# Five activation tiles of a two-layer backbone kernel begin 32 bytes further in SBUF

## The chip, the cores and the metric

The kernel runs on one core of a Trainium2 chip. The metric is the device time of one execution in microseconds (us); the time before is the median of three runs. The profile is of one further execution on the chip.

## What is computed

The reference is a diffusion backbone of two layers on 256 latent and 256 context tokens of width 1024, in float32. Each layer is a half-weighted SwiGLU feed-forward step (width 2816), a token mixer (neighbourhood attention, a bidirectional linear recurrence and a Fourier mix behind one input projection and in front of one output projection) and a second feed-forward step. Each step is modulated by columns made from a conditioning vector, and each is followed by a layer norm over the residual. Cut to what matters here:

```python
def swiglu(h, wg, wu, wd):
    return (jax.nn.silu(h @ wg) * (h @ wu)) @ wd

def ffn_sublayer(xs, m, j, wg, wu, wd, g, b):
    y = MACARON * swiglu(modulate(xs, m, j), wg, wu, wd)
    return residual_post_norm(xs, m[3 * j + 2] * y, g, b)

for l in range(DEPTH):
    x_lat = ffn_sublayer(x_lat, m_lat, 0, ...)
    x_ctx = ffn_sublayer(x_ctx, m_ctx, 0, ...)
    y_lat, y_ctx = hybrid_mixer(modulate(x_lat, m_lat, 1), modulate(x_ctx, m_ctx, 1), ...)
    x_lat = residual_post_norm(x_lat, m_lat[5] * y_lat, ...)
    x_lat = ffn_sublayer(x_lat, m_lat, 2, ...)
    ...
```

## The kernel before, in words

Activations are kept transposed: features on the 128 partitions, the 512 tokens (256 of the context, then 256 latent ones) along the free dimension, eight chunks of features one behind the other. A product with a weight matrix is made in three parts so that float32 accuracy is kept with a rounded type: an operand is split into a high part (`hH`, `aH`, `whi`) and a remainder (`hL`, `aL`, `wlo`), and high by high, high by remainder and remainder by high are summed in PSUM. All this is issued by `mmh` at line 420: a matmul there has a block of weights of 128 by 128 as its stationary operand and 256 columns of an activation tile as its moving operand; for every matmul the weights are loaded anew. With both streams, two such matmuls (context, latent) follow each other with the same weights. In the rows, `gu` are the products of the feed-forward steps' two input matrices, `dn` those of their output matrix, `pj`, `head` and `wo` those of projections.

Weights come by DMA in tiles of 128 by 1024 (`raw`), five of them in turn, ScalarE rounds them (`whi`, line 282) and VectorE or GpSimd subtracts (`wlo`, line 620). Their order is a fixed sequence (`seq`), and the order of the mixer's pieces is written out by hand (`ORDER`); neither has to do with addresses.

Where a tile lies in SBUF follows from the order in which the pools and their tiles are made. The pool `const` is the first. Its first tile begins at byte 16,512 of each partition, which leaves 128 when divided by 512. Five tiles of 16,384 bytes follow one another there: `xT` (the residual), `hH` and `hL` (the input of a product), `aH` and `aL` (the input of the next). Then come `cs` (5,632 bytes: the identity matrix and Fourier tables), `vT` (1,536), `onesD` (512), and `one_c` (one column of ones, 4 bytes, which takes 32). All sizes but the last are multiples of 512, so each of these nine begins at remainder 128. Every slice that a matmul of line 420 takes of `hH`, `hL`, `aH` or `aL` begins a multiple of 1,024 bytes into its tile, so it too begins at remainder 128. Behind `one_c` lie small tiles and then the other pools; `raw`, `whi`, `wlo`, the pool `acc` (with the queries of the attention, `q`) and the pool `scr` (with its keys, `k`) all begin at remainder 448, and a weight block of 512 bytes too.

`one_c` is read as a bias of one column, twice in each piece `sq` of the mixer (line 930).

Of the kernel before, what the change touches and what calls it, by code (L numbers as in the profile page):

```python
# [11 lines left out]
F32 = mybir.dt.float32  # L12
# [53 lines left out]
def kernel(ctx: ExitStack, tc: tile.TileContext, x, cx, vecs, cst, bias, w_ada,  # L66
# [3 lines left out]
    const = ctx.enter_context(tc.tile_pool(name="const", bufs=1))  # L70
# [10 lines left out]

    V, S, G, PE = nc.vector, nc.scalar, nc.gpsimd, nc.tensor

    xT = const.tile([128, KD, 512], F32, name="xT")
    hH = const.tile([128, KD, 512], F32R, name="hH")
    hL = const.tile([128, KD, 512], F32R, name="hL")
# [7 lines left out]
    SN = cs[:, 896:1408].rearrange("p (a b) -> p a b", a=2)  # L94
    vT = const.tile([128, V_ROWS], F32, name="vT")
    onesD = const.tile([128, 128], F32, name="onesD")
    one_c = const.tile([128, 1], F32, name="one_c")
    pick = const.tile([128, 2, 2], F32R, name="pick")
    scol = const.tile([128, KD, 2], F32, name="scol")
    bmean = const.tile([128, 6], F32, name="bmean")  # L100
# [1409 lines left out]
```

## Time and profile before

| | |
|---|---|
| median of 3 runs | 1820.0 us (1819.4 to 1820.87) |
| the profiled execution's own time | 1820.95 us |
| its span, first to last instruction | 1819.2 us |
| TensorE matmul busy (PE) | 1729.1 us, 95% |
| TensorE weight load busy (PEld) | 1658.0 us, 91% |
| VectorE busy (DVE) | 1282.1 us, 70% |
| ScalarE busy (ACT) | 742.0 us, 41% |
| GpSimd busy (POOL) | 460.2 us, 25% |
| mean granted TensorE clock | 0.982 of full |
| moved by DMA | 253.32 MB, mean 139 GB/s |

Busy time of an engine is the time in which at least one of its instructions runs; matmuls overlap each other, so their mean durations do not add up to it. How often TensorE can begin a matmul is read from the starts of successive ones, or from a piece of the chain that holds nothing else: its length divided by its count. This distance is called the pitch below.

### The profile page before, as it was taken

The page shows a single profiled execution, that of the slowest core. Times are in us where ns is not written, and L with a number is a line of the kernel's source. Part 1 is how long each engine was busy: PE and PEld are TensorE (multiplying, and loading weights), DVE is VectorE, ACT ScalarE, POOL GpSimd, SP SyncE. Part 2 cuts the span into 40 slices and gives each one's busy share as a digit, 9 for nine tenths or more (in the row PEclk, how much of TensorE's full clock was granted, in tenths as well). Part 3 has the DMA queues.
Part 4 walks back from the last instruction along what each step waited for, and adds up shares of the span by engine and source line. Part 5 has one row for each costly group of instructions (what it writes and reads, how often), then busy time and mean ns, then how long its engine had stood idle before and what let it go on. Part 6 is the DMA issues. An engine that isn't in the chain of part 4 may idle for free.

```text
span 1819.2 us, 33814 instructions
## 1 busy us (share of the span) xinstructions
PE 1729.1 (95%) x14145; PEld 1658.0 (91%) x14145; DVE 1282.1 (70%) x1857; ACT 742.0 (41%) x1191; POOL 460.2 (25%) x326
## 2 busy tenths in 40 slices
PE   6899999999899999999999999999999989989997
PEld 4789999998798899999999989999999878879997
DVE  6899799956685678866565568865653768676565
ACT  4322232233757545422222364223223466655443
POOL 3435133243542044110101140100000466150000
PEclk8999999999999999999999999999999999999999
DMA  8367555643213225644454326665563232357662
GB/s 292 98 187 204 151 171 169 185 126 93 71 47 93 70 71 147 185 140 143 127 172 120 90 59 185 178 183 159 179 184 95 82 105 70 105 158 214 183 198 83
DMA packets 375080, 253.32 MB, mean 139 GB/s; under 512 B 8144, under 2 KB 336336, under 8 KB 374928
## 3 DMA queue, kind: packets, MB, share of 16 engines
q1 hardware_dynamic: 373856, 248.81, 46.4%
q8 instruction: 111, 1.82, 0.4%
q0 software_dynamic: 1072, 2.36, 0.4%
q14 instruction: 41, 0.34, 0.1%
HBM read 250.09 MB, written 1.05 MB: 138 GB/s over the span
## 4 chain that ended last, share of the span: by engine, by line
PE 74%; DVE 17%; ACT 5%; issue 2%; DMA 1%; POOL 0%; SPq 0%; DVEq 0%; ACTq 0%
PE gu L420 39%; PE dn L420 21%; PE head L420 5%; DVE acc L319 3%; PE pj L420 3%; PE wo L420 2%; DVE wlo L620 1%; DVE ri L939 1%; DVE h L1324 1%; PE o L1133 1%; DVE aL L620 1%; DVE xl L906 1%; ACT whi L282 1%; DVE xT L754 1%; PE adap L359 1%
## 5 line engine op out<-in xcount | busy, mean ns | idle before, releaser
L420 PE MATMUL gu<-hH,whi 128*128 128x256 f32 x2336 | 493.8, 281 | 8.3 <-ACT hH L1326 6.8
L420 PE MATMUL gu<-hH,wlo 128*128 128x256 f32 x2336 | 492.2, 280 | 6.8 <-DVE wlo L620 6.4
L420 PE MATMUL gu<-hL,whi 128*128 128x256 f32 x2336 | 492.2, 280 | 1.7 <-POOL hL L620 0.9
L282 ACT CAST whi<-raw 128x1024 fp32r<-128x1024 f32 (+1 forms) x319 | 318.8, 1025 | 177.6 <-PE dn L420 70.8
L420 PEld LDWEIGHTS gu<-hH,whi 128*128 128x128 f32 x2336 | 372.0, 190 | 13.0 <-ACT hH L1326 7.3
L420 PEld LDWEIGHTS gu<-hH,wlo 128*128 128x128 f32 x2336 | 371.9, 190 | 7.8 <-DVE wlo L620 7.2
L620 DVE TENSOR_TENSOR wlo<-raw,whi 128x1024 fp32r<-128x1024 f32 (+2 forms) x250 | 313.2, 1256 | 88.0 <-ACT whi L282 79.9
L420 PEld LDWEIGHTS gu<-hL,whi 128*128 128x128 f32 x2336 | 370.7, 190 | 2.5 <-DVE hL L620 1.4
L620 POOL TENSOR_TENSOR wlo<-raw,whi 128x1024 fp32r<-128x1024 f32 (+2 forms) x110 | 217.0, 1979 | 440.2 <-ACT whi L282 414.8
L319 DVE SCALAR_TENSOR_TENSOR acc<-raw,scol,acc 128x512 f32<-128x512 f32 x337 | 291.4, 912 | 1.0
L420 PE MATMUL dn<-aH,whi 128*128 128x256 f32 x1280 | 285.0, 282 | 6.0 <-DVE xT L754 2.9
L420 PE MATMUL dn<-aL,whi 128*128 128x256 f32 x1280 | 280.7, 279 | 0.3 <-DVE aL L620 0.3
L420 PE MATMUL dn<-aH,wlo 128*128 128x256 f32 x1280 | 280.8, 279 | 0.0
L420 PEld LDWEIGHTS dn<-aH,whi 128*128 128x128 f32 x1280 | 208.4, 189 | 11.1 <-DVE xT L754 4.5
L420 PEld LDWEIGHTS dn<-aH,wlo 128*128 128x128 f32 x1280 | 208.0, 189 | 0.2
L420 PEld LDWEIGHTS dn<-aL,whi 128*128 128x128 f32 x1280 | 207.4, 188 | 0.7 <-DVE aL L620 0.7
L767 ACT CAST aH<-pr 128x512 fp32r<-128x512 f32 (+1 forms) x88 | 50.0, 568 | 369.0 <-DVE pr L766 369.0
L766 DVE TENSOR_TENSOR pr<-sg,gu 128x512 f32<-128x512 f32 (+1 forms) x84 | 51.6, 614 | 166.0 <-PE gu L420 111.1
L754 DVE SCALAR_TENSOR_TENSOR xT<-dn,gate,xT 128x256 f32<-128x256 f32 x174 | 78.0, 478 | 83.5 <-PE dn L420 83.0
L381 POOL TENSOR_TENSOR fold<-fold 128x512 f32<-128x512 f32 x24 | 49.3, 2054 | 267.1 <-DVE fold L313 267.1
L420 PE MATMUL pj<-hH,whi 128*128 128x256 f32 x384 | 84.7, 289 | 5.3 <-ACT pt L1102 2.8
L364 ACT COPY rows<-adap 2x512 f32<-2x512 f32 x31 | 17.5, 575 | 162.2 <-PE adap L359 162.2
(267 smaller groups left out, 2377.4 us busy)
## 6 DMA issues: line engine op xcount, KB each, us to landing
raw<-in_w_ada_dram SPq DMA_DIRECT2D x136, 512.0 KB, 4.6
raw<-in_ff_gate_dram SPq DMA_DIRECT2D x88, 512.0 KB, 4.1
raw<-in_ff_up_dram SPq DMA_DIRECT2D x88, 512.0 KB, 4.7
raw<-in_ff_down_dram SPq DMA_DIRECT2D x64, 448.0 KB, 4.0
raw<-in_w_in_dram SPq DMA_DIRECT2D x36, 512.0 KB, 3.9
raw<-in_ff_down_dram SPq DMA_DIRECT2D x32, 512.0 KB, 4.4
raw<-in_w_out_dram SPq DMA_DIRECT2D x16, 512.0 KB, 3.6
in<-in_w_ada_dram SPq DMA_DIRECT2D x8, 512.0 KB, 6.7
```

Of the source, the lines that this page charges most:

```text
L282: S.copy(h_[:, :n], t[:, :n])
L319: V.scalar_tensor_tensor(out=a[:, st], in0=t[:, kk * 512:(kk + 1) * 512], scalar=sc_, in1=a[:, st], op0=ALU.mult, op1=ALU.add)
L359: PE.matmul(pp[0:2, :], lhsT=pick[:, n - 1], rhs=parts[:, i], start=(i == 0), stop=(i == 1))
L381: G.tensor_tensor(out=a[:, 0], in0=a[:, 0], in1=a[:, 1], op=ALU.add)
L420: PE.matmul(o[:, c], lhsT=w, rhs=X[:, k, c], start=first and i == 0, stop=last and i == len(halves) - 1)
L620: (eng or V).tensor_tensor(out=dst_l, in0=src, in1=dst_h.bitcast(F32), op=ALU.subtract)
L754: V.scalar_tensor_tensor(out=xT[:, j, a:b], in0=ps[:, a:b], scalar=gate[:, st, j:j + 1], in1=xT[:, j, a:b], op0=ALU.mult, op1=ALU.add)
L766: V.tensor_tensor(out=pr[:, c], in0=sg[:, c], in1=up[:, c], op=ALU.mult)
L767: S.copy(aH[:, m, c], pr[:, c])
L906: V.scalar_tensor_tensor(out=t3[:, :, off:], in0=s3[:, :, :256 - off], scalar=w[tp], in1=t3[:, :, off:], op0=ALU.mult, op1=ALU.add)
L939: V.reciprocal(gates[c, d][0], gates[c, d][0])
L1133: PE.matmul(o[c][r, a:b], lhsT=vk[c][:, x_ * 128 + 64 * p_:x_ * 128 + 64 * p_ + 64], rhs=pt[c, p_, h][:, kc * 256:(kc + 1) * 256], start=( ...
```

## The change

`one_c` is made first in the pool instead of ninth. It takes 32 bytes at 16,512, so `xT`, `hH`, `hL`, `aH`, `aL`, `cs`, `vT` and `onesD` begin 32 bytes further, the activation tiles at byte 16,544 and its successors, all at remainder 160 by 512. The place that `one_c` leaves is filled by the shift: `pick` and everything behind it, all weight tiles included, stay where they were. No instruction is added, removed, moved or given another shape; on each engine the order is the same.

```diff
     V, S, G, PE = nc.vector, nc.scalar, nc.gpsimd, nc.tensor
 
+    one_c = const.tile([128, 1], F32, name="one_c")
     xT = const.tile([128, KD, 512], F32, name="xT")
     hH = const.tile([128, KD, 512], F32R, name="hH")
     hL = const.tile([128, KD, 512], F32R, name="hL")
@@ -94,7 +95,6 @@
     SN = cs[:, 896:1408].rearrange("p (a b) -> p a b", a=2)
     vT = const.tile([128, V_ROWS], F32, name="vT")
     onesD = const.tile([128, 128], F32, name="onesD")
-    one_c = const.tile([128, 1], F32, name="one_c")
     pick = const.tile([128, 2, 2], F32R, name="pick")
```

## Rows read from the trace of the kernel before

**Rows 1.** The page: busy time of the engines, and the chain's shares.

```profile
PE 1729.1 (95%) x14145; PEld 1658.0 (91%) x14145; DVE 1282.1 (70%) x1857; ACT 742.0 (41%) x1191; POOL 460.2 (25%) x326
...
PE 74%; DVE 17%; ACT 5%; issue 2%; DMA 1%; POOL 0%; SPq 0%; DVEq 0%; ACTq 0%
```

**Rows 2.** Chain's longest pieces: start, length in us, engine, tile, line, matmuls.

```profile
328.19 54.40 PE gu L420 x480
...
934.04 79.15 PE gu L420 x672
...
1321.10 56.53 PE gu L420 x480
1452.54 18.84 PE head L420 x160
...
1690.35 38.08 PE gu L420 x336
...
1747.46 38.08 PE gu L420 x336
```

**Rows 3.** Groups by line and form, PE: count, busy us, mean ns, idle before.

```profile
L420 PE MATMUL gu<-hL,whi 128*128 128x256 f32 x2336 | 492.2, 280 | 1.7 <-POOL hL L620 0.9 <-DVE hL L620 0.8
...
L420 PE MATMUL dn<-aL,whi 128*128 128x256 f32 x1280 | 280.7, 279 | 0.3 <-DVE aL L620 0.3
...
L420 PE MATMUL pj<-hL,whi 128*128 128x256 f32 x384 | 82.8, 284 | 0.0
...
L420 PE MATMUL head<-hL,whi 128*128 128x256 f32 x256 | 39.7, 283 | 0.0
...
L420 PE MATMUL wo<-aL,whi 128*128 128x256 f32 x144 | 33.6, 279 | 0.0
```

**Rows 4.** Windows (us, busy us and count by engine, PEclk, DMA share, GB/s).

```profile
324.00:382.00 58.00, 58.00 (x514) 58.00 (x514) 53.67 (x69) 15.23 (x19) 17.36 (x7) 1.00 0.63 184
921.00:1041.00 120.00, 120.00 (x1021) 120.00 (x1020) 66.73 (x91) 33.93 (x44) 12.21 (x6) 1.00 0.41 121
...
528.04:528.68 0.64, 0.64 (x4) 0.64 (x4) 0.64 (x1) 0.64 (x1) 0.64 (x1) 0.50 0.00 0
```

**Rows 5.** Timeline of PE at 528 us: start, us, line, operation, tiles, count.

```profile
528.04 0.42 PE L1042 MATMUL sc<-k,q 128*128 128x256 f32 x1
528.26 0.42 PE L1041 MATMUL sc<-k,q 128*128 128x256 f32 x1
528.47 0.41 PE L1042 MATMUL sc<-k,q 128*128 128x256 f32 x1
528.68 0.63 PE L420 MATMUL pj<-hH,whi 128*128 128x256 f32 x2
```

**Rows 6.** Timeline of PE at 591 us, four score matmuls and the next.

```profile
591.53 0.28 PE L1041 MATMUL sc<-k,q 128*128 128x256 f32 x1
591.65 0.28 PE L1042 MATMUL sc<-k,q 128*128 128x256 f32 x1
591.76 0.28 PE L1041 MATMUL sc<-k,q 128*128 128x256 f32 x1
591.88 0.28 PE L1042 MATMUL sc<-k,q 128*128 128x256 f32 x1
592.00 0.40 PE L1041 MATMUL sc<-k,q 128*128 128x512 f32 x1
```

**Rows 7.** Timeline of PE: conditioning sums with weights of four columns.

```profile
18.42 0.62 PE L1293 MATMUL adap<-wlo,scol 128*4 128x512 f32 x2
18.88 0.62 PE L1293 MATMUL adap<-whi,scol 128*4 128x512 f32 x2
```

**Rows 8.** Timeline of PE: the same sums from activation tiles.

```profile
44.30 0.62 PE L1293 MATMUL adap<-aL,scol 128*4 128x512 f32 x2
44.76 0.63 PE L1293 MATMUL adap<-aH,scol 128*4 128x512 f32 x2
45.23 0.62 PE L1293 MATMUL adap<-aL,scol 128*4 128x512 f32 x2
```

**Rows 9.** Timeline of PE at 583 us: transposes.

```profile
583.52 1.47 PE L1100 MATMUL ptp<-cs,P 128*128 128x128 f32 x12
584.83 0.60 PE L1100 MATMUL ptp<-cs,Pc 128*128 128x128 f32 x4
```

**Rows 10.** Groups by line, PE, in the windows 921 to 1041 and 1642 to 1780 us.

```profile
L420 PE MATMUL gu<-hL,whi 128*128 128x256 f32 x224 | 44.6, 281 | 0.0
...
L420 PE MATMUL gu<-hL,whi 128*128 128x256 f32 x287 | 79.2, 276 | 0.0
```

## The prediction

> **What bounds the kernel now.** I read the page first. TensorE is busy for 1729.1 of 1819.2 us and holds 74% of the chain that ended last; VectorE, next, holds 17% [rows 1]. So the question is how fast TensorE can begin its matmuls. The chain cut into pieces shows that there are two speeds. The piece at 328.19 us has 480 matmuls in 54.40 us, 113.33 ns each; the one at 1690.35 has 336 in 38.08 us, again 113.33 ns. The piece at 934.04 has 672 in 79.15 us, 117.78 ns each, and those at 1321.10 and 1452.54 have 117.77 and 117.75 ns [rows 2]. The matmuls have the same shape, and the granted clock is 1.00 in the windows around the first and the third of these pieces [rows 4]. So something that is not the clock decides between 113.33 and 117.78 ns, and holds its decision for hundreds of matmuls.
>
> How much lies at each? Line 420 issues 2336, 1280, 384, 256 and 144 matmuls for each of three products [rows 3], 13,200 in all. Of the chain's 25 longest pieces, 14 have a pitch of 117.75 ns or more (3,733 matmuls), nine have 113.3 to 114.5 ns (2,424), and two are mixed; [rows 2] has some of either kind. I don't know the other 7,043 from this view.
>
> **What a pitch is made of.** At half the granted clock (0.50 at 528 us [rows 4]) four score matmuls of 256 columns begin 0.21 to 0.22 us apart [rows 5]. Half of that is 0.105 to 0.11 us, and so the full clock could do about 107 ns. Reading four bytes a column at the full clock costs 6 to 11 ns more. Transposes, which read 128 columns, begin 109 ns apart: twelve in the 1.31 us from 583.52 to 584.83 [rows 9].
>
> Does the place of the operands matter? Two rows say no. The conditioning sums, 512 columns with weights of only four columns, begin two in 0.46 us when they read `whi` or `wlo`, at remainder 448 [rows 7]; read from `aH` and `aL`, at remainder 128, they take 0.46 to 0.47 us [rows 8]. So the moving operand's remainder alone, as between 448 and 128, does nothing, and the excess is there without a real weight load beside it. One row says perhaps. The attention's scores have moving operand and weights both at remainder 448, a distance of 0; four of them begin 0.12, 0.11, 0.12 and 0.12 us apart, 0.47 us in all and 117.5 ns on average [rows 6]. That is the slow pitch. Line 420 reads activations at 128 and weights at 448, a distance of 320, and there the fast pitch is held over 480 matmuls [rows 2].
>
> **The change, part by part.** No instruction, wait or DMA is added or moved; every cost lies in the speed of those that are there.
>
> 1. *Moving operands of line 420 begin at 160, weights stay at 448.* The distance falls from 320 to 288. On a circle of 512 the old one is 192 from zero and the new one 224, nearer the opposite point, 256. If a meeting of the two streams decides the pitch, this is the better side. The price is unknown, and I bound it by rows. Slow matmuls known from the long pieces, all made fast: 3,733 x 4.45 ns = 16.6 us. The share in those pieces, 3,733 of 6,157 or 61%, applied to all 13,200 is 8,000 x 4.45 ns = 35.6 us. The short pieces behind each interruption are nearest in kind to neither, so I take the middle, 26 us. That gives 1820.95 - 26 = 1795, and 1 us less against the median of 1820.0: **1794 us**.
>
> 2. *ScalarE, VectorE and GpSimd write and read `xT`, `hH`, `hL`, `aH` and `aL` from 160.* No row has these operations at a start of this kind; I cost them at nothing. What covers them is TensorE: VectorE is busy 53.67 of 58.00 us while TensorE runs at the fast pitch without a gap [rows 4]. If all VectorE work there were 5% slower it would need 56.4 us and still fit; from 8% on it would not, and each further per cent would cost 0.5 us in such a window. At 921 us VectorE has 66.73 of 120.00 us [rows 4], so a faster TensorE finds its weights ready. What comes late next, where the pitch falls, is VectorE's `wlo`, but only in windows like that at 324 us, and that one already runs fast.
>
> 3. *`cs`, `vT`, `onesD` and `one_c` move too.* They feed transposes and a few sums. The dearest of these rows is at 109 ns a transpose; I cost this at nothing.
>
> The Trainium skill has a rule against any such effect: "TensorE: Matmul & The Clock Gate", section "Step-by-step: what each phase is for", says that TensorE has two independent SBUF read ports, so that loading the next weights takes no read bandwidth from the running matmul. By that rule the sum is 0 and the time 1820 us; the scores' 117.5 ns against 113.33 speak mildly against it, the sums with four columns for it.
>
> **The rivals.**
>
> *No change, 1820 us.* The level is chosen by when TensorE starts again after an interruption, and addresses have no part. For it: the two equal rows of conditioning sums, and levels that last from one interruption to the next [rows 2]. Against it: the scores. The price is 0. The Trainium skill's "SBUF — State Buffer", section "Door 1: The DMA port swizzle", counts lines of 16 bytes, and 128 and 160 are both whole lines; by that rule nothing would happen either, and no row here shows a start that is not a whole number of such lines in a long stream.
>
> *The fast level is lost: slower, 1846 us.* This is the mechanism of step 1 with its sign turned: the distance of 320 may be what allows the fast level at all, and 288 may be one of those that don't, as 0 seems to be. It decides at one point: whether long pieces at 113.33 ns still exist. The price is the fast matmuls x 4.45 ns: 2,424 known are 10.8 us, all but the known slow ones, 9,467, are 42 us; the middle is 26 us.
>
> *Starts off 64 bytes cost a piece more: 1909 us.* 160 is not a multiple of 64, while all moving operands that the rows show (128, 448) are. If the 6.6 ns between 107 and 113.33 are one read of 16 columns too many, an odd start would add another: 13,200 x 6.67 ns = 88 us. Nothing in the rows speaks for reads of that size but this one difference; an excess that grows with the columns (two matmuls of 512 take 0.46 us, not 0.43) speaks against a fixed cost per matmul.
>
> *The excess goes altogether: 1729 us.* If the meeting of both streams is all that costs and the new distance avoids it, the pitch falls to the transposes' 109 ns: half of 13,200 by 4.3 ns and half by 8.8 ns is 86 us or, by the shares of the long pieces, 93 us. I take 91. Against it: the sums with hardly any weights have the excess too.
>
> **How the numbers follow.** A measurement of this kernel can tell about 0.2% from no change, 3.6 us. Chances: fewer slow matmuls, as forecast, 0.38 (1785 to 1804, by the two ends of step 1); no change 0.28 (1816 to 1824); fast level lost 0.20 (1831 to 1863); all excess gone 0.07; a piece more per start 0.07. Faster: 0.38 + 0.07 = 0.45; within 0.2%: 0.28; slower: 0.20 + 0.07 = 0.27. Cases of both signs hold most of the chance; the likeliest one's own range is 1785 to 1804. To hold eight in ten, the range reaches to the others: from 1774, which takes in a part of the case in which the excess goes (half of its 91 us), to 1856, which takes in most of the lost fast level; the two extremes are left out.
>
> **What would show it.** Right: the mean duration of matmuls in group rows of line 420, now 279 to 284 ns [rows 3], falls towards the 276 ns that it has in a window of the fast pitch alone, against 281 ns in one of the slow pitch [rows 10]; the chain's long pieces stand at 113.33 ns, and the counts and shapes of all groups are the same. VectorE's and ScalarE's mean durations stay as they are. No change would show the same mix of 113.33 and 117.78; a lost fast level would show no long piece below 117.7 ns; a piece more per start would show 119 ns or more everywhere. A pitch near 109 would mean that I held the excess for a property of the stream where it was one of the pair. The forecast is wrong in its ground if the levels change and the scores and conditioning sums, whose operands haven't moved, change with them, or if another engine's durations explain the difference.

## The result, and the profile after the change

The changed kernel takes 1853.1 us (median of four runs, 1851.34 to 1854.22) against 1820.4 for the kernel before, measured beside it. The ratio is 1.0175 [1.0157, 1.0193]: slower by 32.7 us. The forecast was 1794 us, with a range from 1774 to 1856. The time lies in the range, but on the side of a rival that had been given a chance of 0.20.

The page of the changed kernel: span, busy time of the engines and, after the line of dots, the chain's shares.

```profile
span 1850.4 us, 33814 instructions
...
PE 1763.1 (95%) x14145; PEld 1691.5 (91%) x14145; DVE 1285.0 (69%) x1857; ACT 743.0 (40%) x1191; POOL 457.0 (25%) x326
...
PE 75%; DVE 17%; ACT 5%; issue 2%; DMA 0%; POOL 0%; SPq 0%; DVEq 0%; ACTq 0%
```

The counts are those of [rows 1]. TensorE's busy time grew by 34.0 us, VectorE's by 2.9, ScalarE's by 1.0, and GpSimd's fell by 3.2. So the time lies on TensorE. The longest pieces of the chain, of the same products as in [rows 2] (start, length, engine, tile, line, matmuls), say of what kind it is:

```profile
331.98 56.80 PE gu L420 x480
...
948.25 79.52 PE gu L420 x672
...
1340.84 56.80 PE gu L420 x480
1475.28 18.93 PE head L420 x160
...
1716.83 39.76 PE gu L420 x336
...
1776.47 39.76 PE gu L420 x336
```

Divide length by count: 118.33 ns in every one but `head`, at 118.31. In [rows 2] there were two pitches, 113.33 and 117.78. Now there is one, and it is neither of them. The first piece grew by 2.40 us, the two of 336 by 1.68 each (5.0 ns a matmul); the pieces that had been slow, at 948 and 1340, grew too, by 0.37 and 0.27 us (0.55 ns a matmul). The means of the groups by line and form rose accordingly, where [rows 3] had 280, 279, 284, 283 and 279 ns:

```profile
L420 PE MATMUL gu<-hL,whi 128*128 128x256 f32 x2336 | 497.2, 282 | 1.8 <-DVE hL L620 1.0 <-POOL hL L620 0.8
...
L420 PE MATMUL dn<-aL,whi 128*128 128x256 f32 x1280 | 284.0, 281 | 0.0
...
L420 PE MATMUL pj<-hL,whi 128*128 128x256 f32 x384 | 82.8, 283 | 0.0
...
L420 PE MATMUL head<-hL,whi 128*128 128x256 f32 x256 | 40.2, 285 | 0.0
...
L420 PE MATMUL wo<-aL,whi 128*128 128x256 f32 x144 | 33.9, 281 | 0.0
```

They rose by 2 ns where the pitch rose by 2.85, and `pj`, which has waits and half-clock stretches in it, even fell. A mean duration is a poor measure of a pipelined engine; the pitch is the thing to read.

So that the pitch is known for more than the long pieces, I took all pairs of successive matmuls of line 420 from the trace and the distance between their starts, 13,094 in either kernel. Those of 112 to 126 ns are the full-clock stream; the rest are waits, stretches at half clock and short gaps.

```
              in the stream, mean pitch    at 115 ns or less   other distances   sum
before        12,788 x 115.46 ns           53%                 95.5 us           1572.0 us
after         12,826 x 118.31 ns            4%                 86.2 us           1603.6 us
```

The difference of the sums, 31.6 us, is close to that of the spans, 31.2. The pitch alone would have cost 13,094 x 2.85 ns = 37.3 us, so 5.7 us came back. (The other distances fell by 9.3 us, but 38 of them passed into the stream, where they still cost time.) In the trace, all of TensorE's waits fell from 77.4 to 75.2 us in sum, and the stretches at half clock from 68.1 to 61.8 us, half of which is time lost; that a slower TensorE waits less for the others fits this, but no run takes it apart.

What had not moved kept its speed. The scores, `k` against `q`, in the timeline of TensorE after the change (start, us, line, tiles, count):

```profile
598.86 0.28 PE L1041 MATMUL sc<-k,q 128*128 128x256 f32 x1
598.98 0.28 PE L1042 MATMUL sc<-k,q 128*128 128x256 f32 x1
599.10 0.28 PE L1041 MATMUL sc<-k,q 128*128 128x256 f32 x1
599.21 0.28 PE L1042 MATMUL sc<-k,q 128*128 128x256 f32 x1
599.34 0.39 PE L1041 MATMUL sc<-k,q 128*128 128x512 f32 x1
```

Four begin in 0.48 us, where [rows 6] had 0.47: equal, in a view that is rounded to 0.01. The transposes, whose identity did move, still begin 108 to 109 ns apart, twelve in 1.30 us where [rows 9] had 1.31:

```profile
590.86 1.47 PE L1100 MATMUL ptp<-cs,P 128*128 128x128 f32 x12
592.16 0.60 PE L1100 MATMUL ptp<-cs,Pc 128*128 128x128 f32 x4
```

### The profile page after: what moved, and what is told of

Read it like the earlier page. It is cut to its first block, busy times and chain, and to the rows that moved or that the text cites. A ratio compares the mean times of both kernels' runs of the same rounds, so it can differ in the third digit from the quotient of the medians.

```text
span 1850.4 us, 33814 instructions
## 1 busy us (share of the span) xinstructions
PE 1763.1 (95%) x14145; PEld 1691.5 (91%) x14145; DVE 1285.0 (69%) x1857; ACT 743.0 (40%) x1191; POOL 457.0 (25%) x326
## 4 chain that ended last, share of the span: by engine, by line
PE 75%; DVE 17%; ACT 5%; issue 2%; DMA 0%; POOL 0%; SPq 0%; DVEq 0%; ACTq 0%
PE gu L420 39%; PE dn L420 20%; PE head L420 5%; PE pj L420 3%; DVE acc L319 3%; PE wo L420 2%; DVE wlo L620 1%; PE o L1133 1%; DVE ri L939 1%; DVE h L1324 1%; DVE xT L754 1%; DVE xl L906 1%; DVE aL L620 1%; PE adap L359 1%; DVE fold L313 1%
## 5 line engine op out<-in xcount | busy, mean ns | idle before, releaser
L420 PE MATMUL gu<-hH,whi 128*128 128x256 f32 x2336 | 499.1, 283 | 6.8 <-ACT hH L1326 6.8
L420 PE MATMUL gu<-hH,wlo 128*128 128x256 f32 x2336 | 497.3, 282 | 5.5 <-DVE wlo L620 5.3
L420 PE MATMUL gu<-hL,whi 128*128 128x256 f32 x2336 | 497.2, 282 | 1.8 <-DVE hL L620 1.0
L282 ACT CAST whi<-raw 128x1024 fp32r<-128x1024 f32 (+1 forms) x319 | 318.6, 1025 | 181.9 <-PE dn L420 78.8
L620 DVE TENSOR_TENSOR wlo<-raw,whi 128x1024 fp32r<-128x1024 f32 (+2 forms) x250 | 314.2, 1260 | 86.1 <-ACT whi L282 78.1
```

The source lines that it names most:

```text
L282: S.copy(h_[:, :n], t[:, :n])
L420: PE.matmul(o[:, c], lhsT=w, rhs=X[:, k, c], start=first and i == 0, stop=last and i == len(halves) - 1)
L620: (eng or V).tensor_tensor(out=dst_l, in0=src, in1=dst_h.bitcast(F32), op=ALU.subtract)
```

## The experiments

Three theories stood against each other. *Pair*: the distance between the weights and the moving operand decides the pitch. *Own*: the moving operand's remainder alone decides it. *Restart*: only the moment at which TensorE begins again after an interruption decides it. Twelve kernels were run; each full kernel was timed beside the kernel before (1820.4 to 1821.3 us). Distances are "weights minus moving operand" in bytes: 320 before, 288 after.

### x1: a sweep of places with nothing else running

The model is left out: a kernel with the three products of line 420 alone, 192 matmuls of 256 columns for each setting, in four groups. The weights begin `wo` bytes and the moving operands `xo` bytes behind the starts of their tiles, whose sizes are multiples of 512; so the distance is `wo` where the weights are shifted, and 512 less `xo` where the moving operands are. After each group come two sums of 512 columns whose weights are two columns.

```diff
+SETS = [("m" + chr(97 + i), 32 * i, 0) for i in range(16)]
+SETS += [("w" + chr(97 + i), 0, 32 * i) for i in range(1, 16)]
...
+        for c, xo, wo in SETS:
...
+                    for q, (w, t) in enumerate(((w1, XH), (w2, XH), (w1, XL))):
+                        for h in range(2):
+                            m = t[:, a + k * 512 + h * 256:a + k * 512 + h * 256 + 256]
+                            mm(o[:, h * 256:h * 256 + 256], w, m, ...)
```

> A kernel that leaves the model out: only matmuls of line 420's kind (256 columns, a new weight block for each, three products, no waits between them), four groups of 48 per setting, and behind each group two sums of 512 columns with two-column weights. In turn the moving tiles begin 0, 32, ... 480 bytes further (tiles ma to mp) with the weights fixed, then the weights with the moving tiles fixed (wb to wp), then 4, 8 and 16 bytes (fa to fc), then four pairs: 32 and 320 (ba), 32 and 352 (bb), 160 and 480 (bc), 64 and 320 (bd). Theory 'pair' (the distance between weights and moving operand decides): the pitch changes with the distance, equal distances give equal pitches (bb and bc like wk, 113.3 among them; ba at 118.3), and moving the weights by 32 costs as much as moving the activations. Theory 'own' (a moving operand off 64 bytes costs, wherever the weights are): mb, md, mf and every second one at 118.3, the even ones at 113.3 to 117.8, and the whole weights' series like ma. Theory 'restart' (addresses have no part): all settings show the same mix of 113.3 and 117.8.

Pieces of the chain in this kernel, one group each, at distances 288 (`mh`), 256 (`mi`), 64 (`mo`) and 320 (`wk`):

```profile
203.43 5.75 PE mh L37 x48
...
228.67 5.83 PE mi L37 x48
...
379.77 5.55 PE mo L37 x48
385.84 5.73 PE mo L37 x48
...
655.59 5.54 PE wk L37 x48
```

A piece of 48 is some 0.08 us longer than 48 pitches, since it ends with one matmul's tail; differences are exact. Mean pitch in ns, from the starts of successive matmuls:

```
distance           0      32     64     96    128    160    192    224
moving shifted   119.8  118.3  114.7  118.1  118.6  119.8  117.7  117.0
weights shifted    -    118.3  113.6  118.0  119.6  119.9  117.8  117.3
distance         256     288    320    352    384    416    448    480
moving shifted   119.8  118.2  114.7  118.1  118.6  119.8  117.7  117.0
weights shifted  119.8  118.3  113.6  118.0  119.6  119.9  117.8  117.3
```

Read the two rows of either block together: whichever operand is moved, the pitch goes with the distance, to about 1 ns. Read the blocks against each other: the second repeats the first, so the circle has 256 bytes and not 512. On it, 320 is the same as 64, the best of the eight steps, and 0 and 256 are among the worst. Two levels far apart show only at 64 and 320: single groups lie at 113.3 to 114.0 ns or at 117.7 to 117.8, as the two pieces of `mo` show, 0.18 us apart; elsewhere in the table the groups of a setting differ by 1.5 ns at most. Moving both operands keeps the pitch of the distance: 114.6 and 115.8 ns for two settings at 320, 118.3 at 288, 119.9 at 256. The sums with two columns of weights, whose distance changes with the moving operand alone, took 230 to 233 ns at all sixteen of its places: their rate doesn't show the distance.

Three settings shifted the moving operand by less, a distance of 4, 8 or 16 bytes below zero: 4 bytes gave 123.2 ns, 8 bytes 117.6, 16 bytes 116.4; at 4 bytes the sums of 512 columns rose to 237 ns as well.

### x2, x3, x4: the distance in the kernel itself

x2 is the changed kernel with 32 bytes more in front of the weights: activations at 160, weights at 480, distance 320 again. The pad also moves every pool behind the constants, `q` and `k` with them.

```diff
     bmean = const.tile([128, 6], F32, name="bmean")
...
+    const.tile([128, 8], F32, name="pad")
```

> The changed kernel with 32 bytes more behind the pool of constants, so that weights begin at 480 and activations at 160: the distance is 320 again, as before the change. Theory 'pair': 1820 us and long pieces at 113.33 ns. Theory 'own': 1853 us, all long pieces at 118.3 ns. Theory 'restart': neither address matters, 1820 to 1853 with a mix.

It took 1820.0 us, ratio 0.9998 [0.9987, 1.0009]. Both levels are back, 59% of the stream at the fast one (its line 421 is 420 of the others):

```profile
329.44 56.53 PE gu L421 x480
936.78 79.15 PE gu L421 x672
...
1321.37 54.40 PE gu L421 x480
...
1746.43 38.08 PE gu L421 x336
```

The activations stand at 160 and nothing is lost: *own* falls.

x3 is the kernel before with that pad alone: activations stay at 128, weights and the pools behind them go to 480, distance 352.

```diff
+    const.tile([128, 8], F32, name="pad")
```

> The kernel before with only the 32 bytes behind the constants: activations stay at 128, weights begin at 480, distance 352. Theory 'own': 1820 us, since the moving operands are where they were. Theory 'pair': not 1820; either sign, at most 1790 to 1853. Theory 'restart': 1820.

1846.9 us, ratio 1.0144 [1.0126, 1.0162], mean pitch 118.12 ns, 11% of it fast. No activation moved, and the kernel became slower by 26.5 us. *Restart* alone can't say why. Two of the pieces, of 117.33 and 118.66 ns:

```profile
330.13 56.32 PE gu L421 x480
...
1710.14 39.87 PE gu L421 x336
```

x4 makes `pick` early as well: activations at 192, weights at 448, distance 256, towards which step 1 had taken the change to be a gain.

```diff
+    one_c = const.tile([128, 1], F32, name="one_c")
+    pick = const.tile([128, 2, 2], F32R, name="pick")
     xT = const.tile([128, KD, 512], F32, name="xT")
...
-    one_c = const.tile([128, 1], F32, name="one_c")
-    pick = const.tile([128, 2, 2], F32R, name="pick")
```

> The kernel before with activations 64 bytes further (192), weights at 448, distance 256. Theory 'own' (only starts off 64 cost): 1820 us and 113.33 ns pieces. Theory 'pair': a time of its own, between 1790 and 1853; by the forecast's picture of a circle it would be the best distance, which the changed kernel already speaks against. Theory 'restart': 1820.

1867.9 us, ratio 1.0262 [1.0245, 1.0279]: the slowest of all. Its pieces stand at 120.0 ns:

```profile
333.56 57.60 PE gu L420 x480
...
955.20 80.64 PE gu L420 x672
...
1730.69 40.32 PE gu L420 x336
```

Together with the kernel before and after, four distances lie in the order of the sweep: 320 at 115.46 ns, 352 at 118.12, 288 at 118.31, 256 at 119.91.

### x5: steps of four bytes around 320

The model is left out again; the weights were shifted from 288 to 352 bytes in steps of 4, eight groups each, with a different interruption in front of each group. Three settings more put the weights of the second product elsewhere, and three the moving operand of the third.

```diff
+SETS = [("w" + chr(97 + i), 0, 0, 288 + 4 * i, 288 + 4 * i) for i in range(17)]
+SETS += [("l" + chr(97 + i), 0, 0, 320, w) for i, w in enumerate((304, 336, 512))]
+SETS += [("x" + chr(97 + i), 0, o, 320, 320) for i, o in enumerate((16, 48, 128))]
...
+                mm(p[0:2, 0:64 + 12 * g], WH[:, 0:2], XH[:, 0:64 + 12 * g], True, True)
```

> The model is left out again: the stream of line 420's matmuls as in the first sweep, eight groups per setting, each behind sums of another length, so that the stream starts in different ways. Weights 288 to 352 bytes further in steps of 4 with the moving tiles fixed (wa to wq; wi is 320), then three settings in which only the low weights stand elsewhere (304, 336, 512: la, lb, lc), and three in which only the low moving tile does (16, 48, 128 further: xa, xb, xc), the rest at distance 320. Theory 'pair': wa at 118.3 and wi at 113.4 or, after some of the starts, 117.8, as in the first sweep; in between a minimum of a width that tells how near the kernel before is to its edge. If one distance holds 113.4 after every start, it is better than the kernel before's. A low part that stands elsewhere gives a mixture of its own distance's pitch and of 113.4. Theory 'own' would have starts off 8 or 16 bytes dear and all others alike.

Mean pitch in ns, by distance:

```
288 118.3   292 119.9   296 119.2   300 117.8   304 117.8   308 117.3
312 117.9   316 119.6   320 115.1   324 118.4   328 118.3   332 113.4
336 119.1   340 120.0   344 115.2   348 118.5   352 117.9
```

Pieces at 320 (`wi`) and at 332 (`wl`):

```profile
420.88 5.70 PE wi L36 x48
427.07 5.54 PE wi L36 x48
433.11 5.73 PE wi L36 x48
...
569.69 5.50 PE wl L36 x48
575.68 5.52 PE wl L36 x48
581.70 5.53 PE wl L36 x48
```

At 320 the level depends on how the group began; five of eight were fast. At 332 all eight were, 113.3 to 113.6 ns. Two more means hide two levels: at 308 four groups lie at 114.3 to 114.4 ns and four at 120.1, at 344 four at 113.3 to 113.9 and four at 116.7. At 288, 304 or 328 all eight agree to 0.2 ns. So *restart* has a part, and only where the distance allows two levels. Where one of the three products had another distance than the other two, the means were 119.9, 117.9 and 117.6 ns (weights of the second at 304, 336 and 512) and 117.2, 116.6 and 117.6 ns (moving operand of the third at 16, 48 and 128). They are no mixture of 113.4 with the pitch of the one distance, as had been expected: one product at another distance slows its neighbours. With the second's weights at 304, the slowest was the third product, 125.6 ns, whose own operands stand at 320.

### x6, x7, x8: which of the shifted tiles matter

x6 makes `one_c` between `hL` and `aH`, so that only `aH`, `aL`, `cs`, `vT` and `onesD` move. Products `gu`, `pj` and `head` keep the distance 320, `dn` and `wo` get 288.

```diff
     hL = const.tile([128, KD, 512], F32R, name="hL")
+    one_c = const.tile([128, 1], F32, name="one_c")
     aH = const.tile([128, 8, 512], F32R, name="aH")
...
-    one_c = const.tile([128, 1], F32, name="one_c")
```

> Only aH, aL, cs, vT and onesD begin 32 bytes further; xT, hH and hL stay at 128. Theory 'pair': dn and wo (4,272 of 13,200 matmuls) run at the distance 288, 118.3 ns throughout, and gu, head and pj (8,928) keep their mixture of 113.3 and 117.8. By their share of the 32.7 us, 10.6 us: about 1831 us. If writing these tiles were what costs (ScalarE, VectorE), their instructions' mean durations would be longer.

1825.7 us, ratio 1.0027 [1.0016, 1.0039], where about 1831 had been expected. Two pieces, one of either kind:

```profile
328.76 54.42 PE gu L420 x480
...
1671.09 22.71 PE dn L420 x192
```

`dn` stands at 118.30 ns and `wo` at 118.26 on average, as after the change. But `gu` has 73% of its stream at the fast level, before 54%, and `head` 64%, before 6%. Something else in the shift helps, and the candidates are the tiles behind `aL`.

x7 moves `xT` behind `one_c`: `hH` to `aL` stay at 128, `xT`, `cs`, `vT` and `onesD` move to 160.

```diff
-    xT = const.tile([128, KD, 512], F32, name="xT")
     hH = const.tile([128, KD, 512], F32R, name="hH")
...
+    one_c = const.tile([128, 1], F32, name="one_c")
+    xT = const.tile([128, KD, 512], F32, name="xT")
     cs = const.tile([128, 1408], F32, name="cs")
...
-    one_c = const.tile([128, 1], F32, name="one_c")
```

> Only xT, cs, vT and onesD begin 32 bytes further (at 160), and hH, hL, aH, aL stay at 128. Theory 'pair': 1820 us, no change, pitches of 113.3 and 117.8 as before; transposes at 109 ns. A theory in which another engine's reads and writes of shifted tiles cost: over 1824 us, with longer instructions on xT.

1806.9 us, ratio 0.9914 [0.9898, 0.9931], 87% of the stream fast: the expectation missed. x8 tells `xT` from the rest: only `cs`, `vT` and `onesD` move.

```diff
     aL = const.tile([128, 8, 512], F32R, name="aL")
+    one_c = const.tile([128, 1], F32, name="one_c")
     cs = const.tile([128, 1408], F32, name="cs")
...
-    one_c = const.tile([128, 1], F32, name="one_c")
```

> Only cs (the identity and the Fourier tables), vT and onesD begin 32 bytes further; xT and all operands of line 420 stay. This takes apart the run in which xT moved too and which took 1807 us. Theory 'pair, and the level is chosen at each restart': the share of matmuls at 113.3 is changed by whatever runs between two pieces of the stream, the transposes that read the identity among them; then this run is at 1807 us like that one, with 85 to 90% of line 420's matmuls at 113 to 115 ns. Theory 'xT' (its place for ScalarE and VectorE): 1820 us.

1807.0 us, ratio 0.9920 [0.9904, 0.9937]. So no part of `xT` shows, and this is the better version of the kernel: 14.0 us less than before, 46 less than after the change. Its pieces, the first two slow before and fast now:

```profile
931.57 76.16 PE gu L420 x672
...
1310.54 54.40 PE gu L420 x480
...
1734.64 38.08 PE gu L420 x336
```

In the stream 83% is fast, mean pitch 114.10 ns. By the starts, 12,784 x 114.10 ns + 101.2 us of other distances = 1559.9 us, 12.1 less than before; the span is 13.0 us less. `cs` holds the identity that the transposes read, and transposes interrupt the stream; where they leave off, the stream begins again at one level or the other. No run moves `cs` without `vT` and `onesD`, but the trace says where the gain lies. I sorted the stretches of line 420 by what ran on TensorE just before them (a stretch ends at another instruction or a gap of 0.5 us) and counted the distances of 112 to 126 ns and the share of them at 115 ns or less:

```
behind                                          before         x2             x8
29 times: transposes adat (identity and rows)   49% of 7,213   57% of 7,224   98% of 7,138
28 times: sums adap (part and pick)             93% of 1,647   92% of 1,648   87% of 1,707
8 times: sums m (s and onesD)                   10% of   956    6% of   956   38% of   953
```

Of the 3,900 fast distances that x8 has more, 3,407 stand behind the transposes `adat`, which read `cs` and neither `vT` nor `onesD`. Before, nearly each of their stretches is fast from end to end or slow from end to end, 15 of them fast; in x8 26 are. In x2, where the identity and `rows` moved together by 32 bytes, as the stream's operands did, little changed. So the place of the operands of what runs just before a stretch bears on the stretch's level; by what way, no run shows.

### x9 to x12: distance 332 in the kernel

A distance of 332 needs weights that begin 12 bytes later. In these four kernels the weight tiles are slices of one large tile. Some products use other weight values than the reference's there; the 13,094 pairs of successive matmuls of the line and their shapes are the same, so they are evidence on the pitch; on the whole time they are weaker, since a weight that is taken out of turn can hide a wait. In all four, 32 bytes more stand behind the weights, so the pools behind begin at 480.

x9 is the control, without the 12 bytes.

```diff
-    whi_p = ctx.enter_context(tc.tile_pool(name="whi", bufs=5))
-    wlo_p = ctx.enter_context(tc.tile_pool(name="wlo", bufs=5))
+    wring = ctx.enter_context(tc.tile_pool(name="wring", bufs=1))
...
+    def wtile(i):
+        a = 0 + 1024 * (5 * i + place[i])
+        place[i] = (place[i] + 1) % 5
+        return ring[:, a:a + 1024]
```

> Control: the weights' ten buffers lie in one tile and are taken in turn by slices, at the same place and remainder as before (448), distance 320; 32 bytes more stand behind them, so the pools behind begin at 480. Expected by every theory: within 10 us of 1820, pitches 113.3 and 117.8; what differs is the restart mix.

x10 adds the 12 bytes, three columns.

```diff
-        a = 0 + 1024 * (5 * i + place[i])
+        a = 3 + 1024 * (5 * i + place[i])
```

> As the control, but every weight buffer begins 12 bytes further, at 460: distance 332, which held 113.4 ns after all eight kinds of start in the fine sweep. Theory 'pair': line 420 at 113.3 ns nearly everywhere; 47% of 13,200 matmuls less by 4.45 ns each are 27 us, so about 1793 us, and better than both kernels. If the level there is chosen by something other than the distance: as the control.

x11 is x10 with `cs` where x8 has it.

```diff
     aL = const.tile([128, 8, 512], F32R, name="aL")
+    one_c = const.tile([128, 1], F32, name="one_c")
     cs = const.tile([128, 1408], F32, name="cs")
...
-    one_c = const.tile([128, 1], F32, name="one_c")
```

> The same with cs, vT and onesD at 160 as well. Theory 'pair': with only one level left at 332 there is nothing for the restarts to choose, so this is within 4 us of the run without the move of cs. If it is lower by 5 us or more, restarts still decide there too.

x9 took 1820.0 us (ratio 1.0000 [0.9989, 1.0012]), x10 1815.8 (0.9967 [0.9955, 0.9979]) and x11 1814.9 (0.9967 [0.9954, 0.9980]). The stream came out as expected: 75% fast in x9, 95% in x10 and x11 (113.62 and 113.64 ns), and the place of `cs` no longer matters. Behind the transposes x9 is at 99% fast though `cs` stands where it did: there it is `rows` that moved. The time of x10 did not come out; 1793 had been expected. The waits of its TensorE, longest sum first (us, times, longest), show one that the kernel before doesn't have:

```profile
PE gu L427 <- ACT wring L289: 10.3, 1, 10.3
PE head L427 <- ACT hH L641: 9.5, 4, 2.6
```

The control x9 has the same wait of 10.3 us, so it belongs to the slices and not to the distance. Against x9, x10 gained 4.2 us, where 0.84 ns of pitch over 13,094 would give 11.0. Its profile is of its slowest execution, 1820.4 us of 1811.7 to 1820.4.

The slices were handed out in strict rotation, the pools hand out what came free. x12 uses the distance 332 and the pools' own order of buffers.

```diff
-        a = 3 + 1024 * (5 * i + place[i])
+        a = 3 + 1024 * (5 * i + int(next(place[i])))
```

> As the run with every weight buffer 12 bytes further (distance 332), but the ten buffers are taken in the very order in which the pools of the kernel before hand them out, in place of a strict turn, which kept the start waiting 10.3 us for one buffer and let one be written before its last reader. Theory 'pair': 95% of line 420's matmuls at 113.3 to 113.5 as in that run, without its wait: 1820.5 less 47% of 13,200 by 4.45 ns, about 1793 us, and no more than 1800. If the time stays at 1815, a faster TensorE is given back in waits elsewhere, and these would be seen in the waits.

1809.5 us, ratio 0.9940 [0.9927, 0.9954]: another miss. That wait is gone and the stream is at 113.76 ns, 0.34 better than in x8, but the time is no better: 2.5 us more, which is not clear of noise, as the two intervals overlap. Its longest sums of waits:

```profile
PE head L438 <- ACT hH L652: 9.4, 4, 2.6
PE gu L438 <- DVE wring L638: 8.1, 4, 2.9
```

By the starts, 12,754 x 113.76 ns + 108.9 us = 1559.8 us: what the pitch gains over x8 (4.5 us over 13,094) is taken back by the other distances, 340 of them instead of 310, and 108.9 us instead of 101.2. The traces show granted clocks below 1 for 61 us in x8, 71 in x12 and 95 in x10; but also for 68 in the kernel before and 76 in x9, whose streams are slower than that of x8. So a faster stream alone doesn't explain it, and why x12 has more than x8 was not settled.

## Why the prediction was wrong, by its own steps

**The bound and the reading of two speeds held.** TensorE decided, the levels of 113.33 and 117.78 ns were real, and something other than the clock chose between them.

**Step 1 failed at its circle.** It took 512 bytes for the circle, 0 for the worst place and so 256 for the best. The circle has 256 bytes, and 256 is the same place as 0: x1 gave 119.8 ns there, and x4 lost 47.5 us. Nor does the pitch fall with the distance from 0: half way round, at 128, it is 118.6 to 119.6 ns, and the best step, 64, has 118 on either side. Of the eight steps of 32 bytes, 320 was the best, so that each neighbour had to be worse, 288 (1853 us) and 352 (1847 us) alike. The ground, that the pair decides, was right; the direction was guessed from two distances. The scores' 117.5 ns, four starts rounded to 0.01 us, were read well enough: in whole nanoseconds twenty such starts are 118.0 ns apart before and 118.4 after. But one slow place and one fast place don't say where the next is faster. The conditioning sums, the prediction's evidence against, could not have shown the effect either: sums with few columns of weights ran alike at all places in x1. That 1853 us lies in the range doesn't bear step 1 out, since the range had been stretched to take in the rival with the opposite sign.

The price in step 1 came near by luck. It took 61% of the matmuls for slow and, at the other end, only the 3,733 known ones, 28%; the starts give 47%, 6,050 slow distances. By 4.45 ns they are 27 us, beside the 26 between the two.

**The rival that came true** was the lost fast level, 1846 us. Its test, no long piece below 117.7 ns, is met. Its price of 26 us was the middle of 10.8 and 42, by fast matmuls x 4.45 ns. Measured: 53% of the 12,788 distances in the stream are 6,738 at the fast level, and they lost 5.0 ns, not 4.45, because the new level is 118.33 and not the old slow one; the other 6,050 lost 0.55. That makes 33.7 + 3.3 = 37.0 us, close to the 37.3 from the means, of which 5.7 came back.

**Step 2 held.** VectorE's `wlo` subtraction takes 1260 ns on average, before 1256; ScalarE's rounding 1025, as before; VectorE's `xT` update 478, as before. One group grew, twelve operations of line 1032 on tiles that did not move, from 579 to 737 ns, 1.9 us in all; in x4, with larger shifts, it has 608. In the windows of [rows 4], after the change:

```profile
324.00:382.00 58.00, 58.00 (x492) 57.85 (x492) 52.06 (x69) 15.25 (x20) 15.63 (x7) 1.00 0.58 173
921.00:1041.00 120.00, 120.00 (x1014) 119.62 (x1014) 67.13 (x88) 32.30 (x41) 9.61 (x4) 1.00 0.44 129
```

TensorE still runs without a gap, at granted clock 1.00, and does 492 matmuls where it did 514 in the first window, 1014 for 1021 in the second.

**Step 3 was wrong in kind.** A transpose still starts 108 to 109 ns after the one before, but moving `cs`, `vT` and `onesD` is worth 14.0 us by x8: it changes the level at which the stream begins again, mostly behind the transposes. After the change this gain had nothing to act on, since 288 has one level (118.2 to 118.4 ns in every group of x5).

**The other rivals.** "No change" fell with the result itself and with x3, where of line 420's operands the weights alone moved: the level is chosen at a restart, but only where the distance offers two. "A piece more" asked for 119 ns or more everywhere; x2 has activations at 160 and no such pitch. "The excess goes altogether" met nothing: no setting of x1 or x5 had a mean below 113.4 ns.

The Trainium skill's "TensorE: Matmul & The Clock Gate", section "Step-by-step: what each phase is for", gives TensorE two independent read ports, so that the next weights' load takes nothing from the running matmul. These runs don't bear that out: moving the weights alone by 32 bytes, from 320 to 352, made the stream of x1 4.4 ns a matmul slower, and that of x3 2.7 ns. The Trainium skill's "SBUF — State Buffer", section "Door 1: The DMA port swizzle", with lines of 16 bytes, has nothing that would tell starts at 128 from starts at 160. By x2 the start at 160 costs nothing of itself; with the weights left at 448 it costs 1.75%.

What is open: why the circle has 256 bytes, what sets the two levels at 320, why 332 has only the fast one, and how an instruction in front of a stretch picks its level.

## What to carry to other kernels

Where TensorE is the bound, divide the long pieces of the chain by their counts: two pitches for one shape at one clock mean that something besides the clock decides. Then sweep the place of the moving operand against the stationary one in a kernel that does nothing else, in steps of 32 bytes over 256; it takes one run, and its order held in the kernel at all four distances. Steps of 4 bytes then found 332, which steps of 32 pass over. Do not infer a direction from two places, and look at small tiles too: here the move of three of them, the one with the identity in front, was worth 14.0 us.

## What was not expected of the hardware

- A stream of float32 matmuls of 256 columns depends on the distance between its two operands in SBUF with a period of 256 bytes: from 113.6 to 119.9 ns in steps of 32 bytes (x1), and by up to 5.7 ns between neighbours 4 bytes apart (113.4 at 332, 119.1 at 336; x5).
- At the distance 320 there are two stable levels, 113.33 and 117.78 ns, held from one interruption to the next; at 332 all eight groups had the fast one (x5).
- A moving operand shifted by 4 bytes against the weights took 123.2 ns for 256 columns, and 237 for 512 where shifts by multiples of 32 took 230 to 233 (x1).
- Which level a stretch takes depends on what ran just before it: behind the small transposes the fast share went from 49 to 98% when the identity moved by 32 bytes (x8).
